# Reordering the steps of an attention loop: a reciprocal moved up, fill work regrouped into named places, late transposes

## The chip, the cores and the metric

One NeuronCore of a Trainium2 chip runs the whole program. The metric is the device time of one execution in microseconds (us), as the median of several runs. Four engines compute: TensorE (PE) multiplies matrices and transposes into PSUM, VectorE (DVE), ScalarE (ACT) and GpSimd (POOL) do the elementwise work. SyncE (SP) starts most of the transfers. Each engine has its own queue of instructions.

## The reference

A trunk of two layers on 512 tokens with 1024 channels. Layer 0 mixes tokens with a Conformer convolution module, layer 1 with a native sparse attention; each is followed by a dense SwiGLU feed-forward block, and both sub-layers are pre-normalised residuals. The change touches the attention alone:

```python
q = partial_rope(rmsnorm(q, q_gain), positions)          # 16 heads of 64
k = partial_rope(rmsnorm(kv[:, 0], k_gain...), positions) # 3 branches, 4 groups
k_cmp, v_cmp = comp[0], comp[1]                # 31 compressed blocks, by a small MLP
s_c = einsum('bgrqd,bgnd->bgrqn', qc, k_cmp) * scale
p_c = masked_softmax(s_c, cmp_end[None, :] <= t[:, None])
o_c = einsum('bgrqn,bgnd->bgrqd', p_c, v_cmp)
...
p_s = masked_softmax(s_s, tok <= t[:, None])   # selected blocks
p_w = masked_softmax(s_w, mask_w)              # window
return g[0] * o_c + g[1] * o_s + g[2] * o_w    # gates, then @ w_out
```

With 512 tokens there are 8 blocks to select and up to 16 may be chosen, and the window is 512 wide, so the selected and the window branch are both plain causal attention over all tokens with keys and values of their own.

## The kernel before

Tokens lie along the free axis of most tiles. A head pair `j` (0 to 7) holds two heads, `par` 0 and 1. A unit is one head pair in one branch: `us = [(j, br) for j in range(8) for br in (1, 2)]`, 16 units, so an even unit is the selected branch (br 1) and an odd unit the window branch (br 2) of the same head pair.

**A unit's work.** `score(U, t)` takes the 128 queries of token tile t against the keys up to them: two matmuls into a PSUM tile "S", a mask and row maximum on DVE (`peak`, which reads S and writes the masked scores to the tile "Pm" and the maximum to "mx"), and an exponential with row sum on ACT (`power`). For t = 0 one pair of matmuls serves both branches, so the even unit does both peaks and the odd unit only its exponential. `weigh(U, t)` finishes the token tiles t and t+1 of one head: one DVE reciprocal of two row sums, then two POOL multiplications by that and the gate. `flip` transposes weighted blocks on PE into a PSUM tile "T" and copies them to SBUF: key block 2 of both heads in one tile (below T2, copied by ACT), blocks 1 and 3 of the first head and of the second (T1a and T1b, copied by DVE), block 0 of the first and of the second (T0a and T0b, copied by ACT). `values` multiplies the transposed weights with V into a PSUM tile "O", for an even unit after the three matmuls of the compressed branch.

**A step.** The loop over n does three units at once: scores of unit n, transposes of unit n-1, values of unit n-2. Below S(p,t) is the score of head p and token tile t. PE's order in a step is S(0,3) S(0,2) S(0,1), values, S(0,0), T2, first fill, T1a, S(1,3), T1b, S(1,2) S(1,1) S(1,0), second fill, T0a T0b. DVE's order follows from the same lines: a score's peak stands where the score stands.

**The queue of reciprocals.** `power` puts (U, t) for t = 2 and t = 0 into the list `late`, and each `weigh_late()` pops the oldest. So a step has four of them: the pairs of head 0 are weighed around T1b, the pair (1,2) after the last score, and the pair (1,0), the last of the unit, in the next step, after S(0,3) S(0,2) S(0,1) and their three peaks.

**Fill.** `FILL` is a list of work for the head pairs still to come, of which each `run_fill()` takes one entry. For q pair p: `scores` (`psc`, four matmuls of queries with compressed keys, and a DVE operation into `sc`), `move` (the split of q into a high and a low part on POOL, "qh" and "ql"), `stacks` (four SBUF to SBUF transfers from SP into "St"), `soft_a` (a DVE maximum and subtraction, and an exponential on ACT left for later), `soft_c` (a DVE sum, reciprocal and gate product into "cl", and a POOL multiplication), `trans` (four PE transposes into "pct", an ACT copy "pch", and a DVE subtraction "pcl" left for later). Beside them stand `n4` to `n7` (norm of a q tile: a PE broadcast into "bc" and a DVE product "qraw"), `d3`, `d5` (split of a k tile, high part on ACT, low part on POOL), `k3`, `k5` (its eight transfers), `wd`, `w0`, `w1` (load and split of the first output weights: "wh" on ACT, "wl" on DVE).

**Left for later.** `behind(f)` puts f into `later`, and `catch_up()` runs all of it: `pcl`, `wl`, the exponential of `soft_a`, and "ol", the low part of a finished output, which `out_parts()` puts there at the end of each odd step from 3 on. `catch_up()` stands before the values of each step and in each `run_fill()`.

**Order and buffers.** In this part `order[0]` is true, so every instruction of PE, DVE, ACT and POOL keeps the order in which the program writes it; SP's transfers are ordered by the scheduler. PSUM has 8 banks: three for the tag "p2", which all of T, psc, pct and bc share, three for S, two for O. A tile of q splits takes two of four "q2" buffers.

Of the kernel before, what the change touches and what calls it, by code (L numbers as in the profile page):

```python
# [15 lines left out]
ALU = mybir.AluOpType  # L16
# [73 lines left out]
}  # L90
V_BESIDE = (
    (("w r12", "st0", "p2m", "sABCD a1"), ("w sa", "t1", "r13 c1", ""), ("w", "", "", "")),
    (("ga", "w", "s0", "s1 b1"), ("", "s2 s3 w", "gb s4 l", "s5 st1"), ("s6 l", "s7 l", "sc", "")))
EVAC_V = ((1, 3), ())
V_BANK = (2, 3, 0, 1)
STK_P = (0,)

FILL = ("tr0 P1.0  P1.1 P1.2  P1.3 P1.4  n4 P1.5+d3  k3+P2.0 n5  P2.1+d5 P2.2  k5 P2.4  n6 P2.5  P2.3 n7  "
        "P3.0 P3.1  P3.2 P3.3  wd P3.4  P3.5 w0  w1").split()
SQB = 4  # L100
Q2B = 4

# [63 lines left out]
def trunk(ctx: ExitStack, tc: tile.TileContext, A, out):  # L166
    order = [False]
    nc = Engines(tc, order)
# [44 lines left out]
    for z in QV_ORDER:  # L213
        if z < 8:
            add("nw_q", z, 1024)
        else:
            w = VW[z - 8]
# [1119 lines left out]
    def nsa(acc, cosT, sinT, gnext):  # L1337
# [95 lines left out]
        w1 = {}  # L1433
# [17 lines left out]
        ks, oT = [], []  # L1451
        box = {}
# [81 lines left out]
        def catch_up(n=9):  # L1534
            for f in later[:n]:
                f()
            del later[:n]
# [16 lines left out]
                after(z, lead)  # L1554
                lead = lead or z

        def split_1(q, eng):

            hi, lo = (qk.tile([P, T], F32R, tag="q2", name=nm(z), bufs=Q2B) for z in ("qh", "ql"))
            if eng is nc.scalar:  # L1560
                eng.activation(hi, q, AF.Copy)
            else:
                eng.tensor_copy(hi, q)
            nc.gpsimd.tensor_tensor(lo, q, hi, ALU.subtract)
            return hi, lo

        def k_move(c):
            box["k2", c] = split_1(ks[c], nc.scalar)

        def k_stack(c):  # L1570
            br, a = divmod(c, 2)
# [79 lines left out]
        def q_pair(p):  # L1651

            a = p // 2
            sc = qk.tile([P, 4, 2, 64], F32, tag="sc", name=nm("sc"), bufs=1)

            def move(jj):
                box["q2", jj] = split_1(oT[2 * p + jj], nc.gpsimd)

            def stacks(jj):
                S2 = qk.tile([P, 1088], F32R, tag="S", name=nm("St"), bufs=3)  # L1660
                hi, lo = box["q2", jj]
                for par in range(2):
                    hs = slice(par * 64, par * 64 + 64)
                    S = qst[2 * p + jj, par] = S2[:, STK_ASIDE + par * T:STK_ASIDE + par * T + T]
                    nc.sync.dma_start(S[hs].bitcast(F32), hi[hs].bitcast(F32))
                    ls = slice(64 - par * 64, 128 - par * 64)
                    nc.sync.dma_start(S[ls].bitcast(F32), lo[hs].bitcast(F32))

            def scores(jj):
                q = oT[2 * p + jj]  # L1670
                ps = p2.tile([P, 4, 64], F32, tag="p2", name=nm("psc"))
                for t in range(4):
                    pe(nc.tensor.matmul(ps[:, t, :], q[:, t * P:(t + 1) * P], kcb[a], start=True, stop=True))
                nc.vector.scalar_tensor_tensor(
                    sc[:, :, jj, :], ps, -1.0,
                    cc[:, C_CADD:C_CADD + 256].rearrange("p (t n) -> p t n", t=4), ALU.mult, ALU.add)

            def soft_a():
                s3 = sc.rearrange("p t j (h n) -> p (t j h) n", h=2)
                m = qk.tile([P, 16 + APART], F32, tag="cm", name=nm("cm"), bufs=1)[:, :16]  # L1680
                nc.vector.tensor_reduce(m, s3, AX.X, ALU.max)
                nc.vector.tensor_tensor(s3, s3, m.unsqueeze(2).to_broadcast([P, 16, 32]), ALU.subtract)
                sf = sc.rearrange("p t j n -> p (t j n)")
                behind(lambda: nc.scalar.activation(sf, sf, AF.Exp))

            def soft_c():
                s3 = sc.rearrange("p t j (h n) -> p (t j h) n", h=2)
                l = qk.tile([P, 16], F32, tag="cl", name=nm("cl"), bufs=1)
                nc.vector.tensor_reduce(l, s3, AX.X, ALU.add)
                nc.vector.reciprocal(l, l)  # L1690
                r0 = 2 * (p % 2)
                gv = gates[:, :, 8 * a:8 * a + 8].rearrange("p t (h r) -> p t r h", h=2)[:, :, r0:r0 + 2, :]
                lv = l.rearrange("p (t j h) -> p t j h", t=4, j=2)
                nc.vector.tensor_tensor(lv, lv, gv, ALU.mult)
                nc.gpsimd.tensor_tensor(
                    s3, s3, l.unsqueeze(2).to_broadcast([P, 16, 32]), ALU.mult)

            def trans():
                pt = p2.tile([P, T], F32, tag="p2", name=nm("pct"))
                for t in range(4):  # L1700
                    pe(nc.tensor.transpose(pt[:, t * P:(t + 1) * P], sc[:, t].rearrange("p j n -> p (j n)"), ident))
                ph = q3[1].tile([P, T], F32R, tag="pch", name=nm("pch"))
                pl = q3[1].tile([P, T], F32R, tag="pcl", name=nm("pcl"))
                nc.scalar.activation(ph, pt, AF.Copy)
                behind(lambda: nc.vector.tensor_tensor(pl, pt, ph, ALU.subtract))
                pcT[p] = (ph, pl)

            if p == 0:
                return move, scores, stacks, soft_a, soft_c, trans
            return [lambda: (move(0), scores(0)), lambda: (stacks(0), scores(1)), lambda: (move(1), soft_a()),  # L1710
                    lambda: stacks(1), soft_c, trans]

        extra, bcs = {}, {}

        def run(z):
            for f in z.split():
                extra[f]()
# [68 lines left out]
        for e in range(2, 14):  # L1786
# [8 lines left out]
            n = state["next"]  # L1795
# [139 lines left out]
        def weigh_late():  # L1935
            if late:
                weigh(*late.pop(0))
# [13 lines left out]
        def flip(parts, tag, eng):  # L1951

            pt = p2.tile([P, T], F32, tag="p2", name=nm("T"))
            t_ = box["q4"].tile([P, T], F32, tag=tag, name=nm("t"), bufs=2 if tag != "t2" else 1)
            c = 0
            for u, kc in parts:
                n = T - P * kc
                u[kc] = t_[:, c:c + n]
                for t in range(kc, 4):
                    pe(nc.tensor.transpose(pt[:, c:c + P], block(u, t)[:, P * kc:P * kc + P], ident))  # L1960
                    c += P
            if eng is nc.vector:
                eng.tensor_copy(t_, pt)
            else:
                eng.activation(t_, pt, AF.Copy)
# [25 lines left out]
        def out_parts():  # L1991
            if outs:
                j, o = outs.pop()
                h_ = op.tile([P, T], F32R, tag=f"o{j}", name=nm("oh"))
                l_ = oha.tile([P, T], F32R, name=nm("ol"))
                nc.scalar.activation(h_, o, AF.Copy)
                behind(lambda: nc.vector.tensor_tensor(l_, o, h_, ALU.subtract))
                oh.append(h_)
                ol.append(l_)

        us = [(j, br) for j in range(8) for br in (1, 2)]
        N = len(us)
        fill_ = list(FILL)
        U = {}
        oh, ol = [], []

        pairs = {}

        def pair_(p, i):
            if i == 0:  # L2010
                pairs[p] = q_pair(p)
            pairs[p][i]()

        for p in range(1, 4):
            for i in range(6):
                extra[f"P{p}.{i}"] = lambda p=p, i=i: pair_(p, i)
        extra["wd"] = lambda: [w_dma(state["next"] + i) for i in range(3)]
        for i in range(2):
# [2 lines left out]
        extra["l"] = weigh_late  # L2021
        extra["-"] = lambda: None

        def run_fill():
            catch_up()
            if fill_:
                run(fill_.pop(0).replace("+", " "))

        def start(n):
            j, br = us[n]  # L2030
# [23 lines left out]
        for n in range(1, N + 2):  # L2054
            S = n < N
            F = n <= N
            if S:
                start(n)

            def sc_(par, *ts):  # L2060
                if S:
                    for t in ts:
                        score(U[n][par], t)

            sc_(0, 3, 2, 1)
            weigh_late()
            if n > 1:
                catch_up()
                values(U.pop(n - 2))
            sc_(0, 0)  # L2070
            if F:
                ua, ub = U[n - 1]
                flip(((ua, 2), (ub, 2)), "t2", nc.scalar)
            run_fill()
            if F:
                flip(((ua, 1), (ua, 3)), "t1", nc.vector)
            weigh_late()
            sc_(1, 3)
            if F:
                flip(((ub, 1), (ub, 3)), "t1", nc.vector)  # L2080
            weigh_late()
            if n == 1:
                catch_up(1)
            sc_(1, 2, 1, 0)
            weigh_late()
            run_fill()
            if F:
                flip(((ua, 0),), "t0", nc.scalar)
                flip(((ub, 0),), "t0", nc.scalar)
            out_parts()  # L2090
        catch_up()
        order[0] = False
# [202 lines left out]
```

## Time and profile before

| what | value |
|---|---|
| median of 3 runs | 1160.72 us (1159.14 to 1163.09) |
| the profiled execution's own time | 1159.72 us |
| its span, first to last instruction | 1158.0 us |
| PE busy, in the span | 1151.8 us (99%) |
| DVE, ACT, POOL busy | 863.9, 586.8, 404.2 us |
| the attention steps (1 to 17), about | 648.9 to 778.3 us |

The profile names groups by tiles and shapes, since one helper line (L153) records nearly all instructions. In the timelines PEld is the weight load that precedes each matmul: a matmul's end is modelled, so the start of a load is the better clock of where PE is. A note in brackets says how long the engine was idle before an instruction and what ended that.

### The profile page before, as it was taken

To read this page: it belongs to the slowest core of one execution; us is meant where nothing else is said; L and a number is where in the kernel's file an instruction comes from. 1 tells how busy PE (TensorE), PEld (TensorE's weight loads), DVE (VectorE), ACT (ScalarE), POOL (GpSimd) and SP (SyncE) were. 2 spreads that over 40 slices of the span, in tenths; PEclk is the share of its full clock that TensorE was granted. 3 is DMA by queue.
4 is the path that set the end of the run, shared out by engine and by line. 5 is a ranking of instruction groups with operands and counts; after the bars stand their busy time and mean duration, and the time that the engine had idled before them with its cause. 6 is when DMAs were issued, how large, how long until landed. Compare 5 with 4: busy or idle time off the path is not lost.

```text
span 1158.0 us, 21725 instructions
## 1 busy us (share of the span) xinstructions
PE 1151.8 (99%) x8341; PEld 1010.2 (87%) x8341; DVE 863.9 (75%) x1554; ACT 586.8 (51%) x1120; POOL 404.2 (35%) x441
## 2 busy tenths in 40 slices
PE   9999999999999999999999999999999999999998
PEld 7888788899999988998779877768889999998898
DVE  7898787998777567875676778764699877756566
ACT  6322454565555444454333687773455555544443
POOL 1029122054444101233232577752304444430031
PEclk9999999999999999999999999999999999999999
DMA  9745437287777532534373232112736777762342
GB/s 365 272 126 126 97 101 208 91 208 192 192 192 197 156 114 88 162 109 114 89 171 107 56 74 56 38 38 89 202 105 164 205 192 195 192 187 93 108 128 73
DMA packets 86552, 164.27 MB, mean 142 GB/s; under 512 B 36656, under 2 KB 37808, under 8 KB 85680
## 3 DMA queue, kind: packets, MB, share of 16 engines
q1 hardware_dynamic: 66944, 108.52, 30.3%
q0 software_dynamic: 19504, 54.37, 19.8%
q8 instruction: 65, 1.06, 0.4%
q14 instruction: 39, 0.32, 0.1%
HBM read 147.23 MB, written 5.28 MB: 132 GB/s over the span
## 4 chain that ended last, share of the span: by engine, by line
PE 97%; DVE 1%; POOL 1%; issue 0%; ACT 0%; POOLq 0%; ACTq 0%
PE st L153 50%; PE pp L153 30%; PE O L153 3%; PE T L153 3%; PE S L153 3%; PE cpe L153 2%; PE pv L153 2%; POOL Pm L153 1%; PE warm L153 1%; PE psc L153 1%; DVE Pm L153 0%; PE z L153 0%; DVE t L153 0%; PE psq L153 0%; PE rbc L153 0%; PE lng L153 0%
## 5 line engine op out<-in xcount | busy, mean ns | idle before, releaser
L153 PE MATMUL st<-ball,sh 128*128 128x256 f32 x1760 | 304.8, 275 | 0.0
L153 PEld LDWEIGHTS st<-ball,sh 128*128 128x128 f32 x1760 | 264.8, 188 | 1.3 <-ACT c L153 1.0
L153 PE MATMUL st<-ball,sl 128*128 128x256 f32 x880 | 242.1, 275 | 0.0
L153 DVE TENSOR_TENSOR wl<-wr,wh 128x1024 fp32r<-128x1024 f32 (+3 forms) x144 | 178.2, 1237 | 84.5 <-ACT wh L153 84.4
L153 ACT ACTIVATE wh<-wr 128x1024 fp32r<-128x1024 f32 (+3 forms) x144 | 148.8, 1033 | 171.4 <-PE st L153 60.2
L153 POOL DMA_DIRECT2D S<-fw_x x88 | 78.3, 891 | 276.1 <-DVE sl L153 219.5
L153 POOL TENSOR_TENSOR S<-S,wr 128x512 f32<-128x512 f32 x84 | 118.7, 1413 | 147.9 <-DMA wr<-fw_op 119.3
L153 PEld LDWEIGHTS st<-ball,sl 128*128 128x128 f32 x880 | 165.2, 188 | 0.0
L153 PE MATMUL pp<-hh,wh 128*128 128x512 f32 x384 | 153.0, 398 | 0.1
L153 PE MATMUL pp<-hh,wl 128*128 128x512 f32 x384 | 149.8, 390 | 0.0
L153 PE MATMUL pp<-hl,wh 128*128 128x512 f32 x384 | 149.8, 390 | 0.0
L153 DVE TENSOR_TENSOR sl<-S,sh 128x512 fp32r<-128x512 f32 x176 | 117.9, 710 | 30.1 <-ACT sh L153 29.1
L153 PE MATMUL st<-ball,wh 128*128 128x256 f32 x704 | 124.1, 275 | 0.0
L153 ACT ACTIVATE sh<-S 128x512 fp32r<-128x512 f32 x176 | 101.0, 620 | 18.5 <-PE st L153 15.0
L153 PE MATMUL st<-row,wh 128*128 128x512 f32 x352 | 108.4, 389 | 0.0
L153 PEld LDWEIGHTS st<-ball,wh 128*128 128x128 f32 x704 | 106.2, 188 | 0.3
L153 PE MATMUL st<-ball,wl 128*128 128x256 f32 x352 | 96.8, 275 | 0.0
L153 POOL TENSOR_SCALAR Pm<-Pm,mx,gates 128x512 f32<-128x512 f32 (+2 forms) x112 | 72.9, 663 | 45.5 <-DVE mx L153 26.8
L153 PEld LDWEIGHTS pp<-hh,wh 128*128 128x128 f32 x384 | 72.2, 188 | 18.6 <-issue 2.8
L153 PEld LDWEIGHTS pp<-hh,wl 128*128 128x128 f32 x384 | 72.1, 188 | 16.2 <-DVE wl L153 0.9
L153 PEld LDWEIGHTS pp<-hl,wh 128*128 128x128 f32 x384 | 72.3, 188 | 14.6 <-issue 0.2
L153 ACT ACTIVATE c<-st 128x256 f32<-128x256 f32 x132 | 48.8, 379 | 64.8 <-PE st L153 49.5
(266 smaller groups left out, 2169.3 us busy)
## 6 DMA issues: line engine op xcount, KB each, us to landing
S<-fw_x POOLq DMA_DIRECT2D x88, 512.0 KB, 6.1
wr<-fw_in SPq DMA_DIRECT2D x44, 512.0 KB
wr<-fw_or SPq DMA_DIRECT2D x28, 512.0 KB
r<-fw_x SPq DMA_DIRECT2D x44, 256.0 KB
bd<-bands POOLq DMA_DIRECT2D x6, 1280.0 KB, 18.1
wr<-cw_in SPq DMA_DIRECT2D x14, 512.0 KB
wr<-fw_s SPq DMA_DIRECT2D x8, 512.0 KB
wr<-fw_op SPq DMA_DIRECT2D x8, 512.0 KB
```

The costliest lines, as they stand in the source:

```text
L153: z = f(*a, **kw)
```

## The change

The reciprocal of a unit's last pair moves ahead of the first three scores of the next step (and in front of the steps, one more `l`). `FILL` becomes a table by step with up to three places: after T2, after the last score, and a new one after T0b. `catch_up()` no longer stands before the values; it runs in the first two places. The parts of a q pair get names (s0, s1 splits; m0, m1 stacks; c0, c1 scores; a, c softmax; t transposes) and places of their own. The low part of the split of k tile 5 goes from POOL to DVE. In step 16 T1a goes ahead of the values.

```diff
-    (... ("s6 l", "s7 l", "sc", "")))
+    (... ("s6 l", "s7 l", "l sc", "")))
...
-FILL = ("tr0 P1.0  P1.1 P1.2  P1.3 P1.4  n4 P1.5+d3  k3+P2.0 n5  P2.1+d5 P2.2  k5 P2.4  n6 P2.5  P2.3 n7  "
-        "P3.0 P3.1  P3.2 P3.3  wd P3.4  P3.5 w0  w1").split()
+FILL = {
+    1: ("", "tr0 P1.c0", "cu"),
+    2: ("P1.s0", "P1.m0 P1.c1"),
+    3: ("P1.a P1.s1", "P1.m1 n4"),
+    4: ("P1.c", "", "P1.t"),
+    5: ("d3", "k3 n5 P2.c0"),
+    6: ("P2.s0", "P2.m0 P2.c1 d5"),
+    7: ("k5 P2.a P2.s1", "P2.m1 n6"),
+    8: ("P2.c", "", "P2.t"),
+    9: ("", "n7 P3.c0"),
+    10: ("P3.s0", "P3.m0 P3.c1"),
+    11: ("P3.a P3.s1", "P3.m1"),
+    12: ("P3.c", "wd", "P3.t"),
+    13: ("", "w0"),
+    15: ("w1",),
+}
...
-        def split_1(q, eng):
+        def split_1(q, eng, low=nc.gpsimd):
-            nc.gpsimd.tensor_tensor(lo, q, hi, ALU.subtract)
+            low.tensor_tensor(lo, q, hi, ALU.subtract)
-            box["k2", c] = split_1(ks[c], nc.scalar)
+            box["k2", c] = split_1(ks[c], nc.scalar, nc.vector if c == 5 else nc.gpsimd)
...
-            return [lambda: (move(0), scores(0)), lambda: (stacks(0), scores(1)), lambda: (move(1), soft_a()),
-                    lambda: stacks(1), soft_c, trans]
+            return dict(s0=lambda: move(0), s1=lambda: move(1), m0=lambda: stacks(0), m1=lambda: stacks(1),
+                        c0=lambda: scores(0), c1=lambda: scores(1), a=soft_a, c=soft_c, t=trans)
...
-        def run_fill():
-            catch_up()
-            if fill_:
-                run(fill_.pop(0).replace("+", " "))
+        def run_fill(n, i):
+            if i < 2:
+                catch_up()
+            run((FILL.get(n, ()) + ("", "", ""))[i])
...
+            weigh_late()
             sc_(0, 3, 2, 1)
-            weigh_late()
+            if F:
+                ua, ub = U[n - 1]
+            if n == N:
+                flip(((ua, 1), (ua, 3)), "t1", nc.vector)
             if n > 1:
-                catch_up()
                 values(U.pop(n - 2))
             sc_(0, 0)
             if F:
-                ua, ub = U[n - 1]
                 flip(((ua, 2), (ub, 2)), "t2", nc.scalar)
-            run_fill()
-            if F:
+            run_fill(n, 0)
+            if S:
                 flip(((ua, 1), (ua, 3)), "t1", nc.vector)
             weigh_late()
             sc_(1, 3)
             if F:
                 flip(((ub, 1), (ub, 3)), "t1", nc.vector)
             weigh_late()
-            if n == 1:
-                catch_up(1)
             sc_(1, 2, 1, 0)
             weigh_late()
-            run_fill()
+            run_fill(n, 1)
             if F:
                 flip(((ua, 0),), "t0", nc.scalar)
                 flip(((ub, 0),), "t0", nc.scalar)
+            run_fill(n, 2)
             out_parts()
```

More of the change, by code (lines that the diff above doesn't have):

```diff
@@ L92 @@
     (("w r12", "st0", "p2m", "sABCD a1"), ("w sa", "t1", "r13 c1", ""), ("w", "", "", "")),
-    (("ga", "w", "s0", "s1 b1"), ("", "s2 s3 w", "gb s4 l", "s5 st1"), ("s6 l", "s7 l", "sc", "")))
+    (("ga", "w", "s0", "s1 b1"), ("", "s2 s3 w", "gb s4 l", "s5 st1"), ("s6 l", "s7 l", "l sc", "")))
 EVAC_V = ((1, 3), ())
@@ L2002, in nsa @@
         N = len(us)
-        fill_ = list(FILL)
         U = {}
@@ L2009, in pair_ @@
         def pair_(p, i):
-            if i == 0:
+            if p not in pairs:
                 pairs[p] = q_pair(p)
@@ L2014, in nsa @@
         for p in range(1, 4):
-            for i in range(6):
+            for i in ("s0", "s1", "m0", "m1", "c0", "c1", "a", "c", "t"):
                 extra[f"P{p}.{i}"] = lambda p=p, i=i: pair_(p, i)
```

## The prediction

> **What bounds the kernel now.** First the page's head: PE is busy through the whole span, so whatever delays PE in the attention reaches the end. What PE loses there is seen only in the timeline of its weight loads.
>
> ```profile
> span 1158.0 us, 21725 instructions
> PE 1151.8 (99%) x8341; PEld 1010.2 (87%) x8341; DVE 863.9 (75%) x1554; ACT 586.8 (51%) x1120; POOL 404.2 (35%) x441
> ```
>
> Next I read the loads step by step. Step 12 is an even step with no fill work in its first place. From the load of S(0,0) to that of the next S(0,3):
>
> ```profile
> 742.40 0.19 PEld L153 LDWEIGHTS S<-kh,St 128*128 128x128 f32 x1 [0.81 <-issue]
> 743.82 0.69 DVE L153 COPY t<-T 128x512 f32<-128x512 f32 x1 [0.36 <-PE T L153]
> 745.24 0.19 PEld L153 LDWEIGHTS S<-kh,St 128*128 128x128 f32 x1 [0.16 <-DVE mx L153]
> 746.37 0.19 PEld L153 LDWEIGHTS S<-kh,St 128*128 128x128 f32 x1
> ```
>
> The row at 745.24 is S(1,0). It waits for a maximum: three PSUM tiles hold the scores, S(1,0) takes the one of S(1,3), and that is free when DVE has read it, right behind the copy of T1a at 743.82. So the copy of T1a sets S(1,0), 1.42 us later, and DVE had only 0.36 us to spare ahead of it. In step 4 the norm product of `n4` stands there:
>
> ```profile
> 674.92 0.19 PEld L153 LDWEIGHTS S<-kh,St 128*128 128x128 f32 x1 [0.81 <-DVE ol L153]
> 676.14 0.69 DVE L153 TENSOR_TENSOR qraw<-qraw,bc 128x512 f32<-128x512 f32 x1 [0.16 <-PE bc L153]
> 676.74 0.68 DVE L153 COPY t<-T 128x512 f32<-128x512 f32 x1
> 678.15 0.19 PEld L153 LDWEIGHTS S<-kh,St 128*128 128x128 f32 x1 [0.21 <-DVE mx L153]
> ```
>
> The copy comes 1.82 us after S(0,0) instead of 1.42, and S(1,0) 3.23 instead of 2.84: in an even step DVE work between the peak of S(0,0) and the copy of T1a is paid by PE one for one, beyond 0.36 us.
>
> **Part 1: what now stands there.** Before, `catch_up()` ran ahead of the values, where DVE idles while PE multiplies. Now it runs in the first place, which on DVE lies behind the peak of S(0,0), that is behind the values. And `soft_c` moves to the first place of steps 4, 8 and 12, all even. Their lengths on DVE:
>
> ```profile
> 671.59 0.67 DVE L153 TENSOR_REDUCE cl<-sc 128x16 f32<-128x512 f32 x1
> 672.72 0.68 DVE L153 CUSTOM_DVE_ANT_0 Pm<-S,mask 128x512 f32<-128x512 f32 x1
> 756.97 1.21 DVE L153 TENSOR_TENSOR wl<-wr,wh 128x1024 fp32r<-128x1024 f32 x1
> 758.09 0.69 DVE L153 TENSOR_TENSOR ol<-O,oh 128x512 fp32r<-128x512 f32 x1
> ```
>
> `soft_c` takes 672.72 - 671.59 = 1.13 us, wl 758.09 - 756.97 = 1.12, ol 0.60 (the product of the same shape above, back to back). Steps 4, 8, 12: 1.13 + 0.60 - 0.36 = 1.37 each, 4.1 in all, less what the norm products cost steps 4 and 8 before (3.23 - 2.84 less 0.13 of PE's own broadcast, 0.26 each): +3.6. Step 14, wl and ol: +1.36. Steps 6 and 10, ol alone: 0.24 each, +0.5. Lower bound 0 if DVE's lateness were made good within the step; upper bound 6.5, with neither the 0.36 nor the old cost taken off. I take 5.5, since S(1,0) waits for DVE already in both steps shown, with and without such work.
>
> **Part 2: two more PSUM tiles in a second place.** In steps 5 and 9 a broadcast and a `psc` now stand between the last score and T0a (step 9 had the broadcast, step 5 too, without psc). Step 9 before:
>
> ```profile
> 717.59 0.85 PEld L153 LDWEIGHTS T<-cc,Pm 128*128 128x128 f32 x8 [0.81 <-POOL Pm L153]
> 720.80 0.42 PEld L153 LDWEIGHTS T<-cc,Pm 128*128 128x128 f32 x4 [0.18 <-issue]
> 721.18 0.19 PEld L153 LDWEIGHTS S<-kh,St 128*128 128x128 f32 x1
> 721.99 0.17 DVE L153 RECIPROCAL mx<-mx 128x2 f32<-128x2 f32 x1 [0.43 <-ACT Pm L153]
> 722.07 0.67 DVE L153 TENSOR_TENSOR qraw<-qraw,bc 128x512 f32<-128x512 f32 x1
> 726.10 0.97 PEld L153 LDWEIGHTS psc<-kcb,qraw 128*128 128x128 f32 x8
> 726.94 0.48 PEld L153 LDWEIGHTS T<-cc,Pm 128*128 128x128 f32 x4
> ```
>
> bc, psc and T0a hold all three tiles of "p2", so T0b (720.80) waits until the norm product has read bc, and on DVE that stands behind the reciprocal at 721.99, which waits for ACT. It ends at 722.74. With psc's 726.94 - 726.10 = 0.84 T0b would load at 721.64; it loads at about 722.75: 1.1 us lost, in both steps +2.2. Bounds: 0 if a tile were free, 1.5 each if it is psc's evacuation that frees one. In step 1 the same happens with pct and psc, and takes what the earlier reciprocal gives there:
>
> ```profile
> 651.62 0.42 PEld L153 LDWEIGHTS T<-cc,Pm 128*128 128x128 f32 x4 [0.81 <-POOL Pm L153]
> ```
>
> I put step 1 at 0; bounds a gain of 0.8, this wait gone, and a loss of 1.7 (1.1 plus an ACT copy and a DVE subtraction that read pct, less that wait).
>
> **Part 3: ACT ahead of T0's copies.**
>
> ```profile
> 739.78 0.61 ACT L153 ACTIVATE sc<-sc 128x512 f32<-128x512 f32 x1
> 740.92 0.67 PEld L153 LDWEIGHTS O<-t,v 128*64 128x64 f32 x4 [0.29 <-ACT t L153]
> 755.60 0.19 PEld L153 LDWEIGHTS O<-pcl,vch 128*128 128x128 f32 x1 [0.37 <-DVE pcl L153]
> ```
>
> The exponential of `soft_a` now precedes T0's copies in steps 3 and 7 as it did in 11, where the values then waited: +0.2 each. The pcl wait goes, but the 1.0 us of wh then shows there, since PE comes earlier: +0.4. Sum +0.8, bounds 0 and 1.4.
>
> **Part 4: the reciprocal moved up.** It now waits at the head of DVE for the last exponential, and three peaks queue behind it.
>
> ```profile
> 739.14 0.69 DVE L153 CUSTOM_DVE_ANT_0 Pm<-S,mask 128x512 f32<-128x512 f32 x1
> 741.73 0.71 ACT L153 ACTIVATE Pm<-Pm,mx 128x512 f32<-128x512 f32 x1
> ```
>
> The first peak ends at 739.82 and ACT takes it up at 741.73, so a delay of 0.8 us costs nothing; what covers it is ACT's copies of T0. The reciprocal's gain lies where POOL, busy with a split, gave T1b's operand late, in steps 3 and 7 (T2 to the next S(0,3)); there the splits now also come behind it, in the first place:
>
> ```profile
> 666.97 0.86 PEld L153 LDWEIGHTS T<-cc,Pm 128*128 128x128 f32 x8 [0.81 <-POOL qh L153]
> 668.81 0.42 PEld L153 LDWEIGHTS T<-cc,Pm 128*128 128x128 f32 x4 [0.71 <-POOL Pm L153]
> 670.67 0.19 PEld L153 LDWEIGHTS S<-kh,St 128*128 128x128 f32 x1
> 700.97 0.86 PEld L153 LDWEIGHTS T<-cc,Pm 128*128 128x128 f32 x8 [0.81 <-POOL Pm L153]
> 704.90 0.19 PEld L153 LDWEIGHTS S<-kh,St 128*128 128x128 f32 x1
> 682.39 0.19 PEld L153 LDWEIGHTS O<-t,v 128*64 128x64 f32 x2 [0.58 <-ACT t L153]
> 749.96 0.42 PEld L153 LDWEIGHTS T<-cc,Pm 128*128 128x128 f32 x4 [0.81 <-POOL sc L153]
> 753.99 0.19 PEld L153 LDWEIGHTS S<-kh,St 128*128 128x128 f32 x1
> 766.16 0.86 PEld L153 LDWEIGHTS T<-cc,Pm 128*128 128x128 f32 x8 [0.81 <-POOL Pm L153]
> 769.36 0.19 PEld L153 LDWEIGHTS O<-pch,vch 128*128 128x128 f32 x1
> 771.94 0.19 PEld L153 LDWEIGHTS O<-t,v 128*64 128x64 f32 x2 [0.83 <-ACT t L153]
> ```
>
> Steps 3 and 7 take 3.70 and 3.93; with `n4`, `n6` in the second place they become like step 9, 721.18 - 717.59 less the broadcast's 0.13 = 3.46: -0.2 and -0.5. Later transposes: step 4's no longer precede T0's copies, so the wait at 682.39 falls to the usual 0.2: -0.5 with what follows it. Step 13, 4.03 with 0.43 of pct, becomes like step 15, 3.20: -0.4. Step 16 fills the wait at 771.94 with T1a's transposes: -0.4. Gains 2.0; bounds 1.0 and 4.0 (all these notes).
>
> Transfers: SP's order changes, k5 and the stacks issue half a step later, and nothing in the steps' loads waited for a transfer; cost 0, bound 1.0 if k5 came late for S(0,0) of step 8. The low part of k tile 5 on DVE delays step 7's peaks and `soft_a`: +0.2.
>
> ```profile
> 757.15 1.45 POOL L153 TENSOR_SCALAR Pm<-Pm,mx,gates 128x256 f32<-128x256 f32 x1 [0.61 <-DVE mx L153]
> 674.41 0.56 POOL L153 TENSOR_SCALAR Pm<-Pm,mx,gates 128x256 f32<-128x256 f32 x1
> ```
>
> The first ran beside wl, a DVE operation with two SBUF inputs, and took 0.89 longer than the second. The Trainium skill says so (SBUF — State Buffer, "Who interferes with whom"): such an operation and a GpSimd one that reads SBUF exclude each other. By that rule the new DVE subtraction would cost up to 0.9 in place of 0.2, and the sum would be 7.4.
>
> **Sum.** 5.5 + 2.2 + 0.8 + 0.2 - 2.0 = +6.7 us on the profiled execution, 1159.72 (its span 1158.0), so 1166.4. That execution lies 1.0 below the median of the runs, 1160.72; I predict 1166.5 for the median.
>
> **The rivals.** (1) Faster: the values end late enough on PE, or ol, wl and `soft_c` start early enough, that DVE is done before T1a's transposes are. The point that decides is whether the copy of T1a starts within 1.42 us of S(0,0)'s load in steps 4 to 14. Then part 1 is nothing, and the upper gains of 4.0 and step 1's 0.8 stand against half of part 2: 1160.7 - 4.8 + 1.1 = 1157.0, or 1155.9 if T0b finds a tile. For it: DVE is busy 75% only. Against it: the waits for mx in steps 4 and 12, where DVE had 0.36 us to spare or none. (2) Lateness paid back: PE arrives later, so the waits for ACT and POOL in the following odd step shrink; parts 2 and 3 vanish and part 1 halves: 2.7 + 0.2 - 2.0 = +1, 1161.7. (3) Worse: step 1 loses 1.7, k5 comes late, and part 2 reaches its upper bound: +3.5 on the forecast, 1170. That the change doesn't do what it says is bound up with (1): the earlier reciprocal helps only in steps 1, 3 and 7, as elsewhere T1b did not wait for POOL.
>
> **How the numbers follow.** A measurement of this kernel tells about 0.3% from no change, 3.5 us. Forecast 0.54, its own range 1164.3 to 1169.5; (3) 0.10; (2) 0.20, between -3.5 and +3.5; (1) 0.16. So slower 0.64, same 0.20, faster 0.16. The range reaches down into (1) and up into (3): 1157.5 to 1170.
>
> **What would show it.** Right: in steps 4, 8, 12, 14 the note on S(1,0) says DVE mx with over 1 us, with ol or cl back to back before T1a's copy; in steps 5 and 9 T0b idles near 1 us for qraw. The T1b waits for POOL in steps 3 and 7 are gone either way. From S(0,0) of step 12 to the values of step 16 before: 769.36 - 742.40 = 26.96 us; I expect some 29.5 (1.37 in step 12, 1.36 in 14, 0.4 for wh, less 0.4 in 13). Wrong: S(1,0) waits 0.2 as before, or that stretch shortens.

## The result and the profile after

The changed kernel takes 1166.9 us in the median of six runs (1166.14 to 1169.12); six runs of the kernel before have a median of 1160.38 us. The ratio is 1.006, with a 95% interval of 1.0049 to 1.007: slower by 6.5 us. The forecast was 1166.5.

The page of the changed kernel, its head:

```profile
span 1165.0 us, 21740 instructions
PE 1150.4 (99%) x8341; PEld 1011.3 (87%) x8341; DVE 864.6 (74%) x1555; ACT 587.1 (50%) x1120; POOL 400.6 (34%) x440
```

The profiled execution (1166.81 us of its own) is 7.0 longer in its span, and no engine's busy time has grown by more than 0.7 us (the weight loads' by 1.1). PE still counts as 99% busy, but span less PE's busy time has grown from 6.2 to 14.6 us. Where PE stands still is told by the notes on its weight loads. The view of the waits, for those loads in the attention (from 655 to 786 us), columns total us, times, longest; first before:

```profile
PEld S L153 <- DVE mx L153: 0.8, 4, 0.2
```

and after:

```profile
PEld S L167 <- DVE mx L167: 7.6, 10, 1.4
```

Scores that wait for a maximum went from 0.8 to 7.6 us, with single waits of 1.4 where 0.2 was the longest. (In both kernels a load right behind the values carries 0.81 us idle, under changing names; one of these is in the 7.6.) The timelines show which maxima. Step 12 after, which answers to the first fence of the prediction:

```profile
747.04 0.19 PEld L167 LDWEIGHTS S<-kh,St 128*128 128x128 f32 x1 [0.81 <-DVE mx L167]
748.02 0.69 DVE L167 TENSOR_TENSOR ol<-O,oh 128x512 fp32r<-128x512 f32 x1
748.62 0.68 DVE L167 TENSOR_REDUCE cl<-sc 128x16 f32<-128x512 f32 x1
749.72 0.68 DVE L167 COPY t<-T 128x512 f32<-128x512 f32 x1
751.12 0.19 PEld L167 LDWEIGHTS S<-kh,St 128*128 128x128 f32 x1 [1.41 <-DVE mx L167]
...
765.40 1.22 DVE L167 TENSOR_TENSOR wl<-wr,wh 128x1024 fp32r<-128x1024 f32 x1
766.54 0.68 DVE L167 TENSOR_TENSOR ol<-O,oh 128x512 fp32r<-128x512 f32 x1
767.14 0.68 DVE L167 COPY t<-T 128x512 f32<-128x512 f32 x1
768.54 0.19 PEld L167 LDWEIGHTS S<-kh,St 128*128 128x128 f32 x1 [1.45 <-DVE mx L167]
```

The copy of T1a stands behind ol and the three operations of `soft_c`, 2.68 us after S(0,0) instead of 1.42, and S(1,0) follows it by 1.40 us (751.12 - 749.72), where it was 1.42 before. In step 14 it is wl and ol.

The whole attention, counted in both timelines from the first load of the values of one step to that of the next (us):

| values of step | before | after | difference |
|---|---|---|---|
| T2 of step 1 to values of 2 | 6.45 | 6.57 | +0.12 |
| 2 to 3 | 9.28 | 9.24 | -0.04 |
| 3 to 4 | 7.07 | 6.95 | -0.12 |
| 4 to 5 | 9.23 | 10.08 | +0.85 |
| 5 to 6 | 8.42 | 9.01 | +0.59 |
| 6 to 7 | 9.28 | 9.40 | +0.12 |
| 7 to 8 | 7.30 | 8.07 | +0.77 |
| 8 to 9 | 9.24 | 10.07 | +0.83 |
| 9 to 10 | 7.04 | 9.02 | +1.98 |
| 10 to 11 | 10.08 | 9.38 | -0.70 |
| 11 to 12 | 6.57 | 6.56 | -0.01 |
| 12 to 13 | 8.76 | 10.41 | +1.65 |
| 13 to 14 | 7.40 | 6.56 | -0.84 |
| 14 to 15 | 8.80 | 10.46 | +1.66 |
| 15 to 16 | 5.52 | 6.77 | +1.25 |
| 16 to the first output projection | 8.90 | 7.57 | -1.33 |

The sum is +6.78; T2 of step 1 came 0.24 later in this execution, together the 7.02 by which the first output projection is later. Some of the differences are only work that changed its step: 0.84 of `psc` from step 10 to step 9, 0.43 of `pct` from 13 to 12, and T1a of step 16.

In step 5 T0b waits for the norm product, which stands behind the reciprocal:

```profile
688.71 0.17 DVE L167 RECIPROCAL mx<-mx 128x2 f32<-128x2 f32 x1 [0.43 <-ACT Pm L167]
688.79 0.67 DVE L167 TENSOR_TENSOR qraw<-qraw,bc 128x512 f32<-128x512 f32 x1
689.57 0.42 PEld L167 LDWEIGHTS T<-cc,Pm 128*128 128x128 f32 x4 [1.41 <-POOL Pm L167]
689.60 0.63 PE L167 MATMUL T<-cc,Pm 128*128 128x128 f32 x4 [1.20 <-DVE qraw L167]
```

The two notes on one transpose differ: the load names POOL, the matmul DVE's qraw. The product ends at 689.46, 0.14 us ahead of the matmul. In step 9 the same transpose waits 1.41 us by its load and 1.20, for qraw, by its matmul. Which of the two names is right is settled by an experiment below.

Step 7 is the surprise. The prediction's terms for it make 0.3 us less, or 0.17 less with the 0.13 of the broadcast that moved in; it is 0.77 longer:

```profile
700.45 0.89 DVE L167 TENSOR_TENSOR ql<-kraw,qh 128x512 fp32r<-128x512 f32 x1 [0.91 <-ACT qh L167]
702.71 0.86 PEld L167 LDWEIGHTS T<-cc,Pm 128*128 128x128 f32 x8 [0.81 <-POOL Pm L167]
703.21 1.29 POOL L167 TENSOR_TENSOR ql<-qraw,qh 128x512 fp32r<-128x512 f32 x1
703.47 1.58 DVE L167 TENSOR_TENSOR sc<-sc,cm 128x512 f32<-128x512 f32 x1
704.97 0.68 DVE L167 COPY t<-T 128x512 f32<-128x512 f32 x1
705.70 0.19 PEld L167 LDWEIGHTS bc<-qys,er 128*128 128x128 f32 x1 [0.60 <-DVE t L167]
707.03 0.42 PEld L167 LDWEIGHTS T<-cc,Pm 128*128 128x128 f32 x4 [0.64 <-POOL Pm L167]
```

The subtraction of `soft_a` takes 1.58 us, beside a subtraction of POOL, and the copy of T1a waits behind it: 2.26 us after the load of T2. PE pays in two places: the broadcast of `n6` waits 0.60 us for this copy, and T0b waits 0.64 us for POOL, which itself waits for the DVE reciprocal behind the copy. The first row is the moved low part itself. It starts 0.91 us late, behind its high part on ACT, and takes 0.89.

### The profile page after: what moved, and what is told of

The parts are those of the page before. It is cut to its first block, busy times and chain, and to the rows that moved or that the text cites. A ratio compares the mean times of both kernels' runs of the same rounds, so it can differ in the third digit from the quotient of the medians.

```text
span 1165.0 us, 21740 instructions
## 1 busy us (share of the span) xinstructions
PE 1150.4 (99%) x8341; PEld 1011.3 (87%) x8341; DVE 864.6 (74%) x1555; ACT 587.1 (50%) x1120; POOL 400.6 (34%) x440
## 4 chain that ended last, share of the span: by engine, by line
PE 93%; DVE 3%; ACT 2%; issue 1%; POOL 0%; ACTq 0%; DVEq 0%; POOLq 0%
PE st L167 49%; PE pp L167 30%; PE O L167 3%; PE cpe L167 2%; PE S L167 2%; PE T L167 2%; PE pv L167 2%; ACT Pm L167 1%; DVE Pm L167 1%; DVE t L167 1%; PE warm L167 1%; ACT t L167 0%; PE psc L167 0%; PE z L167 0%; PE psq L167 0%
## 5 line engine op out<-in xcount | busy, mean ns | idle before, releaser
L167 POOL TENSOR_SCALAR Pm<-Pm,mx,gates 128x512 f32<-128x512 f32 (+2 forms) x112 | 69.9, 638 | 44.6 <-DVE mx L167 32.2
```

Source lines behind the costliest of these rows:

```text
L167: z = f(*a, **kw)
```

## The experiments

The kernel with a change undone is compared, stretch by stretch, with the changed kernel; the ratios are to the kernel before, run on the same chip. Its median there was 1159.9 to 1160.18 us, up to 0.5 below the 1160.38 above, so a difference between two medians is good to about half a microsecond. The stretches, taken from one profiled execution each, repeat to 0.02 us where nothing was changed.

**Late work ahead of the values again.** `catch_up()` returns to its old place, so that ol and wl run while PE multiplies the values.

```diff
             if n > 1:
+                catch_up()
                 values(U.pop(n - 2))
```

> The changed kernel with catch_up() put back ahead of the values, nothing else. Theory (DVE work behind the peak of S(0,0) is paid by PE): ol and wl leave the stretch, so S(1,0)'s wait for mx falls from 1.41 to 0.8 in steps 4, 8 and 12 (soft_c stays), from 1.45 to 0.2 in step 14 and from 0.31 to 0.2 in 6 and 10: 3.3 us less than the changed kernel, about 1163.6. Rival (the lateness is paid back in the next step): at most 1 us less, about 1166.

Measured: 1163.43 us, ratio 1.0028 (1.0017 to 1.0039), 3.5 us less than the changed kernel. Step 4:

```profile
674.56 0.69 DVE L167 TENSOR_TENSOR ol<-O,oh 128x512 fp32r<-128x512 f32 x1 [0.32 <-ACT oh L167]
675.15 0.19 PEld L167 LDWEIGHTS S<-kh,St 128*128 128x128 f32 x1 [0.81 <-issue]
677.23 0.68 DVE L167 COPY t<-T 128x512 f32<-128x512 f32 x1
678.63 0.19 PEld L167 LDWEIGHTS S<-kh,St 128*128 128x128 f32 x1 [0.81 <-DVE mx L167]
```

The product ol now runs 0.6 us ahead of S(0,0), and the wait of S(1,0) falls from 1.41 to 0.81, by ol's 0.60. The stretches 4 to 5, 8 to 9 and 12 to 13 lose 0.60 each, 14 to 15 loses 1.28 and the two of steps 6 and 10 together 0.32: 3.4 in all.

**The softmax's end in an odd step.** `soft_c` goes to the second place of steps 3, 7 and 11.

```diff
-    3: ("P1.a P1.s1", "P1.m1 n4"),
-    4: ("P1.c", "", "P1.t"),
+    3: ("P1.a P1.s1", "P1.m1 n4 P1.c"),
+    4: ("", "", "P1.t"),
...
```

> The changed kernel with soft_c moved from the first place of steps 4, 8, 12 to the second place of 3, 7, 11; catch_up() stays where the change put it. Theory: S(1,0)'s wait falls from 1.41 to 0.3 in steps 4, 8, 12, 1.1 us each, of which soft_c behind the norm products may take back 0.3 in steps 3 and 7: 2.7 to 3.3 us less, about 1163.9. Rival (paid back): at most 1 us less.

Measured: 1163.86 us, ratio 1.0035 (1.0021 to 1.005), 3.0 less than the changed kernel. Step 4:

```profile
674.39 0.19 PEld L167 LDWEIGHTS S<-kh,St 128*128 128x128 f32 x1 [0.81 <-DVE mx L167]
675.38 0.68 DVE L167 TENSOR_TENSOR ol<-O,oh 128x512 fp32r<-128x512 f32 x1
675.98 0.68 DVE L167 COPY t<-T 128x512 f32<-128x512 f32 x1
677.38 0.19 PEld L167 LDWEIGHTS S<-kh,St 128*128 128x128 f32 x1 [0.32 <-DVE mx L167]
```

The stretches 4 to 5, 8 to 9 and 12 to 13 lose 1.10, 1.09 and 1.03, and the odd ones stay within 0.02: in the second place of an odd step this work is hidden. Ol alone leaves a wait of 0.32. So the two experiments, each with one of the two pieces of work, give back nearly their whole length on DVE.

**The scores of compressed keys in other places.** `psc` of pair 2 goes to the first place of step 5, that of pair 3 to the first place of step 10.

```diff
-    5: ("d3", "k3 n5 P2.c0"),
+    5: ("d3 P2.c0", "k3 n5"),
...
-    9: ("", "n7 P3.c0"),
-    10: ("P3.s0", "P3.m0 P3.c1"),
+    9: ("", "n7"),
+    10: ("P3.s0 P3.c0", "P3.m0 P3.c1"),
```

> The changed kernel with the psc of pairs 2 and 3 out of the second place of steps 5 and 9, into the first place of 5 and 10. Theory (bc, psc and T0a hold all three p2 tiles, T0b waits for the norm product): the waits of 1.41 ahead of T0b go, 1.2 us in each of the two steps: 2.4 us less, about 1164.5. Rival (T0b waits for POOL's weighting, as the note on its load says): the waits stay, within 0.4 us of the changed kernel.

Measured: 1164.57 us, ratio 1.0037 (1.0024 to 1.005), 2.3 less. The stretch 5 to 6 goes from 9.01 to 7.80, and 9 to 11 from 18.40 to 17.03, -1.21 and -1.37. T0b of step 5:

```profile
687.98 0.42 PEld L167 LDWEIGHTS T<-cc,Pm 128*128 128x128 f32 x4 [0.18 <-issue]
```

Counted from the first load of the values of step 5, T0b loads 1.2 us earlier than in the changed kernel (6.36 for 7.57). POOL's three multiplications of that moment start at the same count in both (5.89 for 5.87) and are as long (1.96 us for 1.95), so in the changed kernel too T0b's operand was there in time; only `psc` no longer holds the third PSUM tile. So the load's note of POOL was wrong and the matmul's of qraw right: the wait was for the tile.

**The low part of k tile 5 back on POOL.**

```diff
-            box["k2", c] = split_1(ks[c], nc.scalar, nc.vector if c == 5 else nc.gpsimd)
+            box["k2", c] = split_1(ks[c], nc.scalar)
```

> The changed kernel with the low part of k tile 5 back on POOL. Theory (the subtraction on DVE makes step 7's peaks and soft_a late, and with them the copy of T1a): step 7's stretch from T2 to the next S(0,3), 4.71 us, falls to about 3.6: 1.1 us less, about 1165.8. Rival (soft_a beside the split of q on POOL is what makes it late, whichever engine does k tile 5): the stretch stays above 4.4, no difference.

Measured: 1165.95 us, ratio 1.0049 (1.0034 to 1.0064), 0.95 less. The stretch 7 to 8 is 6.96 us where it was 8.07; all others stay within 0.02. Step 7:

```profile
701.49 1.42 POOL L167 TENSOR_SCALAR Pm<-Pm,mx,gates 128x256 f32<-128x256 f32 x2
701.66 0.93 DVE L167 TENSOR_TENSOR sc<-sc,cm 128x512 f32<-128x512 f32 x1
702.16 0.86 PEld L167 LDWEIGHTS T<-cc,Pm 128*128 128x128 f32 x8 [0.81 <-POOL Pm L167]
703.29 0.69 DVE L167 COPY t<-T 128x512 f32<-128x512 f32 x1 [0.70 <-PE T L167]
703.55 1.29 POOL L167 TENSOR_TENSOR ql<-qraw,qh 128x512 fp32r<-128x512 f32 x1
```

The subtraction takes 0.93 instead of 1.58, and the copy waits for PE again, not PE for the copy. But the run leaves open how much of the 1.11 us was the low part's place in DVE's queue and how much the long subtraction. For that the next run leaves the low part on DVE and takes away what ran beside the subtraction.

**POOL's split out of step 7.** In the changed kernel, `P2.s1` and its transfers go to step 8.

```diff
-    7: ("k5 P2.a P2.s1", "P2.m1 n6"),
-    8: ("P2.c", "", "P2.t"),
+    7: ("k5 P2.a", "n6"),
+    8: ("P2.c P2.s1", "P2.m1", "P2.t"),
```

> After, but POOL's split of the second q tile (P2.s1) and its stacks go from step 7 to step 8, so that in step 7 no POOL subtraction runs beside the softmax subtraction of soft_a on DVE; the low part of k tile 5 stays on DVE. Theory (the two subtractions hold each other): the DVE subtraction that took 1.58 us takes 0.74 to 0.93, the copy of T1a in step 7 comes some 0.65 earlier, and the stretch from the values of step 7 to those of step 8 goes from 8.65 us to about 8.0; the DVE low part of 0.89 us with its wait for its high part then accounts for the rest against 7.53. Rival (the low part on DVE alone made step 7 long, and the 1.58 us is only a late semaphore or the like): the subtraction stays near 1.5 and the stretch stays at 8.6. Step 8 gets the split and is not judged.

Measured in one run: 1166.63 us. Step 7:

```profile
703.12 0.86 PEld L167 LDWEIGHTS T<-cc,Pm 128*128 128x128 f32 x8 [0.81 <-POOL Pm L167]
703.88 0.69 DVE L167 TENSOR_TENSOR sc<-sc,cm 128x512 f32<-128x512 f32 x1
704.49 0.68 DVE L167 COPY t<-T 128x512 f32<-128x512 f32 x1
```

The subtraction takes 0.69 us, and the stretch 7 to 8 is 7.18 (from 8.65 to 7.75 by the expectation's count, which runs between the last rows of the two steps' values). So 0.89 of the 1.11 us was the meeting with POOL's subtraction, more than expected; the DVE subtraction is shorter by the same 0.89. The 0.22 that is left is the low part in DVE's queue: T0b still waits 0.41 us for POOL, where it waits 0.19 with the low part on POOL. The split in step 8 makes POOL late for T2 of step 9, which then waits 0.28 us more, and the stretch 9 to 10 is 0.26 longer. All stretches together are 0.6 us shorter than in the changed kernel; one run's time can't tell that.

**The old kernel without `catch_up()` ahead of the values.**

```diff
             if n > 1:
-                catch_up()
                 values(U.pop(n - 2))
```

> The kernel before with the catch_up() ahead of the values taken out, nothing else: ol, wl and pcl run in the first place. Theory: steps 4 and 8, where the norm product already uses up DVE's spare time, lose 0.6 each, step 12 0.25, step 14 (wl and ol) 1.4, steps 6 and 10 nothing since psc in the first place gives DVE time: 2.8 us more than the kernel before, about 1163.2. Rival (lateness is paid back): at most 1 us more.

Measured: 1162.02 us, ratio 1.0018 (1.0009 to 1.0027), +1.8 in the median; the stretches differ by +0.36, +0.34, +0.15 and +1.28 (those from the values of steps 4, 8, 12 and 14), 2.1 in all, and by nothing in the others. Steps 4 and 14:

```profile
674.84 0.19 PEld L153 LDWEIGHTS S<-kh,St 128*128 128x128 f32 x1 [0.81 <-DVE mx L153]
675.81 0.69 DVE L153 TENSOR_TENSOR ol<-O,oh 128x512 fp32r<-128x512 f32 x1
676.41 0.68 DVE L153 TENSOR_TENSOR qraw<-qraw,bc 128x512 f32<-128x512 f32 x1
677.01 0.68 DVE L153 COPY t<-T 128x512 f32<-128x512 f32 x1
678.41 0.19 PEld L153 LDWEIGHTS S<-kh,St 128*128 128x128 f32 x1 [0.56 <-DVE mx L153]
...
763.51 0.19 PEld L153 LDWEIGHTS S<-kh,St 128*128 128x128 f32 x1 [1.42 <-DVE mx L153]
```

The mechanism holds in the old kernel too, but the size expected was too large: in step 4 ol fills the time in which DVE waited for the broadcast of the norm product anyway, so the copy of T1a comes 2.17 us after S(0,0) instead of 1.82, not 0.60 later. Step 14, where nothing stood before, pays in full.

**The old kernel with the reciprocal alone moved up.**

```diff
-            sc_(0, 3, 2, 1)
             weigh_late()
+            sc_(0, 3, 2, 1)
```

(and one more `l` in front of the steps)

> The kernel before with the reciprocal of the last pair moved ahead of the first three scores, nothing else (and the one more l in front of the steps). Theory (POOL works in order, and the split stands there ahead of the last pair's weighting whatever DVE does): T1b's waits in steps 3 and 7 stay at 0.7 and 0.9; step 1 gains T1b's 0.8 and loses as much at pct, whose multiplication now comes later on POOL: within 0.5 us of the kernel before. Rival (the reciprocal is what makes T1b's operand late): 1.5 us less.

Measured: 1160.46 us, ratio 1.0006 (0.9997 to 1.0015). Every stretch from the values of step 2 on is within 0.02 us of before. T1b of step 3, and pct of step 1:

```profile
651.46 0.42 PEld L153 LDWEIGHTS pct<-cc,sc 128*128 128x128 f32 x4 [1.26 <-POOL sc L153]
...
670.19 0.42 PEld L153 LDWEIGHTS T<-cc,Pm 128*128 128x128 f32 x4 [0.71 <-POOL Pm L153]
```

T1b of step 3 waits 0.71 us for POOL, exactly as before. In step 1 the extra reciprocal puts two more of POOL's multiplications (eight in 4.78 us, where six took 3.81) ahead of the product that pct needs, and pct waits 1.26 instead of 0.30; step 1 as a whole is 0.56 us longer (7.01 for 6.45).

**All dear places mended.** `catch_up()` ahead of the values, `soft_c` in the second places of steps 3, 7 and 11, the low part of k tile 5 on POOL, and no second place with bc and `psc` together:

```diff
-    1: ("", "tr0 P1.c0", "cu"),
-    2: ("P1.s0", "P1.m0 P1.c1"),
-    3: ("P1.a P1.s1", "P1.m1 n4"),
-    4: ("P1.c", "", "P1.t"),
-    5: ("d3", "k3 n5 P2.c0"),
-    6: ("P2.s0", "P2.m0 P2.c1 d5"),
-    7: ("k5 P2.a P2.s1", "P2.m1 n6"),
-    8: ("P2.c", "", "P2.t"),
+    1: ("", "tr0", "cu"),
+    2: ("P1.s0 P1.c0", "P1.m0 P1.c1"),
+    3: ("P1.a cu P1.s1", "P1.m1 n4 P1.c"),
+    4: ("", "", "P1.t"),
+    5: ("d3", "k3 n5"),
+    6: ("P2.s0 P2.c0", "P2.m0 P2.c1 d5"),
+    7: ("k5 P2.a cu P2.s1", "P2.m1 n6 P2.c"),
+    8: ("", "", "P2.t"),
...
```

(steps 9 to 12 in the same way, w0 in the first place of step 13)

> The change with its dear places mended: catch_up() ahead of the values again, psc in the first place of even steps, soft_c in the second place of odd ones, the exponential of soft_a right behind it, wh in the first place of step 13, the low part of k tile 5 on POOL, tr0 alone in step 1's second place. Theory: the losses of the change go and its gains stay (steps 1, 3, 5, 7, 13 and the waits for ACT ahead of the values in 12 and 14): 3.8 us less than the kernel before, about 1156.6. Rival (the waits removed come back elsewhere): within 1 us of the kernel before.

Measured: 1157.56 us, ratio 0.998 (0.9972 to 0.9989): 2.6 us faster than the kernel before, not 3.8. What is missing lies in the values of step 2, which without `psc` in step 1 come too early:

```profile
656.26 0.19 PEld L167 LDWEIGHTS O<-pch,vch 128*128 128x128 f32 x1 [0.73 <-ACT pch L167]
656.99 0.19 PEld L167 LDWEIGHTS O<-pcl,vch 128*128 128x128 f32 x1 [0.54 <-DVE pcl L167]
```

**The same with `psc` back in step 1.**

```diff
-    1: ("", "tr0", "cu"),
-    2: ("P1.s0 P1.c0", "P1.m0 P1.c1"),
+    1: ("", "tr0 P1.c0", "cu"),
+    2: ("P1.s0", "P1.m0 P1.c1"),
```

> The mended version with the first psc back in the second place of step 1 (as in the kernel after), where it covers the wait for pch. Theory: in the mended version the values of step 2 waited 0.73 for pch and 0.54 for pcl since nothing stood between; with psc there, the stretch from the values of step 2 to those of step 3 goes from 9.19 back to 8.35 us, and step 1 (load of T2 to the first load of the values of step 2) from 5.94 to about 6.5, together 0.2 to 0.3 us less, 1157.3 in the median, too small to be told by the times. Rival (psc in step 1 makes T0b wait for a PSUM tile again by its full 1.1): step 1 takes 7.0 and the whole is 0.3 longer.

Measured: 1157.17 us, ratio 0.9975 (0.9965 to 0.9985). The waits of 0.73 and 0.54 are gone: from the values of step 2 to those of step 3, by first loads, 10.58 became 9.23, and step 1 went from 5.94 to 6.57. The gain of 0.7 in the stretches is larger than was expected: the count of 9.19 to 8.35 began at the first load of t, behind the wait of 0.54 for pcl, and so left that wait out. The intervals of the two mended versions overlap, so the runs' times don't tell them apart; both are faster than the kernel before and the changed one. Its step 4:

```profile
675.27 0.19 PEld L167 LDWEIGHTS S<-kh,St 128*128 128x128 f32 x1 [0.81 <-DVE mx L167]
676.69 0.69 DVE L167 COPY t<-T 128x512 f32<-128x512 f32 x1 [0.36 <-PE T L167]
678.10 0.19 PEld L167 LDWEIGHTS S<-kh,St 128*128 128x128 f32 x1 [0.16 <-DVE mx L167]
```

These are the figures of step 12 before: the copy 1.42 us after S(0,0), with 0.36 to spare, and 0.16 of waiting.

## Why the prediction was right, and where it was not

The total came out right, the terms less so: errors of +1.3 and -1.2 us cancelled, so that it came so near is luck. The terms as forecast and as the stretches and experiments give them (us):

| term | forecast | measured |
|---|---|---|
| part 1: DVE work ahead of T1a's copy, even steps | +5.5 | +4.7 |
| part 2: PSUM tiles, steps 5 and 9 | +2.2 | +2.2 |
| part 2: step 1 | 0 | +0.1 |
| part 3: ACT ahead of T0's copies | +0.8 | +0.4 |
| part 4: steps 3, 7, 5, 13, 16 | -2.0 | -1.7 |
| low part of k tile 5 on DVE, its place in the queue | +0.2 | +0.2 |
| the held subtraction in step 7 | none | +0.9 |

The rows sum to 6.8, as the stretches do.

**Part 1** was right in its mechanism and its places (measured: 0.85 and 0.83 in steps 4 and 8, with the broadcast's 0.13 that has left each; 1.65 - 0.43 in 12, 1.66 - 0.40 in 14, 0.12 in 6 and 0.84 - 0.70 in 10): S(1,0) waits 1.41, 1.41, 1.41 and 1.45 us in steps 4, 8, 12 and 14. The forecast was 0.10 to 0.15 us too large in each of the six steps; in steps 6 and 10, where 0.24 each was 0.12 and 0.14, that is about half of it. Its upper bound of 6.5 does not follow from its own words: with neither the 0.36 nor the old cost taken off, the pieces make 3 x 1.73 + 1.72 + 2 x 0.60 = 8.1. In step 12 ol begins 0.98 us after S(0,0) and the copy of T1a follows at 2.68; the forecast had 2.79, from 1.42 + 1.37. The first two experiments show that ol and `soft_c` are paid in their own step: without them that step is shorter and the next one as long as before. Rival 1, that DVE would be done before T1a's transposes, fell by its own point: the copy starts 2.68 us after S(0,0), not within 1.42.

**Part 2** holds in cause and size: 5 to 6 is +0.59, after the shorter wait of the values for t gave back some 0.5, and 9 to 10 is +1.98, of which 0.84 is `psc` itself. The experiment on places gave back 1.21 and 1.37. In step 1 the forecast of 0 stands within 0.1, by the exchange it named: waits of 0.30 ahead of pct and 0.81 ahead of T1b are gone, and psc waits 0.42 and T0b 0.55.

**Part 3**: step 14 pays the 0.40 for wh that was forecast, here in the loads of the values:

```profile
761.38 1.04 ACT L167 ACTIVATE wh<-wr 128x1024 fp32r<-128x1024 f32 x1
762.95 0.19 PEld L167 LDWEIGHTS O<-t,v 128*64 128x64 f32 x2 [0.72 <-ACT t L167]
```

From the first load of its values to S(0,0) step 14 takes 3.95 us, where it took 3.56 with the wait for pcl. The 0.2 each in steps 3 and 7 did not come: the 0.85 by which 4 to 5 grew is the growth from S(0,0) to S(1,0), 4.08 us (679.20 - 675.12) for 3.23.

**Part 4.** Without the broadcast's 0.13, step 3 gained 0.25 and step 13 gained 0.41, as forecast; step 5's values lost their long wait, 0.5. Step 7 would have gained 0.47 (6.96 with the low part on POOL, less 0.13, against 7.30), where 0.5 was forecast. Step 16 gave 0.1 in place of 0.4: T1a ahead of the values now waits for POOL:

```profile
777.33 0.42 PEld L167 LDWEIGHTS T<-cc,Pm 128*128 128x128 f32 x4 [0.84 <-POOL Pm L167]
777.71 0.19 PEld L167 LDWEIGHTS O<-pch,vch 128*128 128x128 f32 x1
```

The forecast asked what T1a would hide there and not whether its operand was ready. The account given for steps 3 and 7 was also off in one point: the reciprocal by itself gives none of their gain. Alone it left T1b's 0.71 in step 3 as it was, and in step 1 it cost 0.56. That the splits' new places do it, alone or together with the reciprocal, is what remains and is not shown; they were not run alone.

**The step that failed** is the cost of the low part of k tile 5, given as +0.2: it measured +1.1. The 0.2 was right for the queue (0.22 by the experiment). What the sum left out is that the later DVE then meets the earlier POOL: its split of the q tile no longer waits behind the low part of k, and its subtraction starts 0.50 us after T2 (before the move 1.39, in the run with the low part on POOL, 703.55 against 702.16), 0.26 ahead of DVE's. The DVE subtraction took 1.58 us in place of 0.69. The Trainium skill names this (SBUF — State Buffer, "Who interferes with whom"): two inputs in SBUF on DVE and a reading GpSimd instruction shut each other out, and the one that issues first goes on to its end. The trace agrees within 0.14 us: POOL's started first and ended at 704.50 (703.21 + 1.29), as long as in the run with the low part on POOL, and DVE's next instruction came 0.47 after that, where the subtraction by itself takes 0.61 to the next instruction (704.49 - 703.88). By that rule the prediction put up to 0.9 on the low part and a sum of 7.4; the rule was the better guide in size, though the instruction that was held is another one, further down DVE's queue.

**The stretch named as a test**, from S(0,0) of step 12 to the values of step 16, is 777.71 - 747.04 = 30.67 us, against 26.96 before. It now holds T1a of step 16 with its wait, 0.84 + 0.38; without these 29.45, where 29.5 was expected. Rival 2, the lateness paid back in the odd steps, would have shown these stretches shorter: 11 to 12 is 6.56 for 6.57, and where an experiment took the lateness out of an even step, the odd step behind it stayed as long. Nothing was paid back. Rival 3's loss in step 1 and its late k5 did not come.

## What to carry to other kernels

Deferred work on an in-order engine should stand where that engine waits anyway: the same 0.60 us product cost nothing ahead of the values and its full length behind them, where DVE still had to get to the peak that frees a PSUM tile of the scores. Count the PSUM tiles that one fill place holds at once, and before moving an operation between DVE and POOL ask what each will then run beside, for the meeting cost four times what the move itself did (0.89 against 0.22). Work that seems to stand idle may be cover, as `psc` of step 1 was for pch and pcl.

## What the runs showed of the hardware

One DVE subtraction of 128x512 with both inputs in SBUF took 0.69 us alone, 0.93 beside POOL's multiplications by a scalar, and 1.58 beside a POOL subtraction of the same shape. And two notes on the same transpose can name different releasers (POOL on its load, DVE on its matmul); in the one place where an experiment could tell, the matmul's was right.
